# Padding the low part of the attention keys to 128 rows, so that both score passes use one full stationary operand

## The chip, the cores and the metric

The kernel runs on one core of a Trainium2 chip. The metric is device time in microseconds (us) of one execution; the kernel before takes 1814.58 us (median of three runs, 1813.2 to 1815.33). The profiled execution is a separate one; its instructions span 1812.8 us.

## The reference, cut to what matters

A two-layer transformer backbone with 256 context and 256 latent tokens of 1024 features. Each layer is a gated feed-forward step (SwiGLU), a mixer, and a second feed-forward step. The mixer holds four differential-attention heads (each with two queries and two keys of 64 dims), four grouped-query heads (two keys of 64 dims) and a recurrent branch. The part that the change touches is the scores:

```
s1 = einsum('bqhd,bkhd->bhqk', q1, k1) * SCALE      # 64 dims per head
s2 = einsum('bqhd,bkhd->bhqk', q2, k2) * SCALE
p  = softmax(s1) - lam * softmax(s2)                # differential heads
s  = einsum('bqngd,bknd->bngqk', q, k) * SCALE      # grouped-query heads
p  = softmax(s)
```

Latent queries see all 512 keys, context queries the 256 context keys; the second layer has latent queries alone. Everything is float32.

## The kernel before, in words

Activations are kept transposed, features on partitions, tokens along the free axis. Products are made in a reduced-precision matmul type (F32R) from exact splits: a value is a rounded high part plus a low part, and a projection is three matmuls (`mm3`, lines 359 to 362: high by high, low by high, high by low). The stationary operand, which the tensor engine loads by a separate instruction ahead of each matmul, is the first factor.

The mixer (line 502) keeps a pair of 64-dim heads (u = 0 and 1) on the 128 partitions. `stack_q` (L602) makes for each u a 128-row tile that holds the high part of q in the 64 rows of that head and the low part in the other 64. `stack_k` (L611) makes three tiles: for each u the high part of k, written twice (L616 and L617), and one shared tile `k[2]` whose rows 0 to 63 hold the low part for u = 0 and rows 64 to 127 that for u = 1 (L618, on VectorE). `scores` (L665) then adds two matmuls in one PSUM bank: L668 takes all 128 rows and gives (qH + qL) kH; L669 takes the 64 rows of that head alone and gives qH kL:

```
s = acc_bank(1, "s")
own = slice(64 * u, 64 * u + 64)
PE.matmul(s[:, 0:nk], q[u][:, a:a + 128], k[u][:, 0:nk], start=True, stop=False)
PE.matmul(s[:, 0:nk], q[u][own, a:a + 128], k[2][own, 0:nk], start=False, stop=True)
```

One call serves 128 queries of one u against nk = 256 or 512 keys. A differential head makes four calls for each stream of queries (two query tiles by two u), and a grouped-query pass four as well. The first layer has two streams (256 keys for context queries, 512 for latent ones), the second has one, with 512 keys. After a call `softmax` runs a maximum on VectorE (L674), an exponential with its sum on ScalarE (L86, called from L676), and a reciprocal (L677); the differential heads then combine two of these on VectorE (L744 to L746), the grouped-query heads scale (L696). `to_keys` transposes on TensorE (L685) and copies out of PSUM on ScalarE (L686), and the product with the values is L702 or L751.

In each layer the attention falls into three stretches: heads 0 and 1 of the differential attention; the two grouped-query passes; heads 2 and 3. The projections for later heads (tiles `m0vp`, `m0q2p`, `m0k2p`, `m0q3p`, `m0k3p`) and the output projection (`m0oy`) are written so that they fill TensorE's waits. A planner orders each engine's instructions at build time; every engine then runs its list in order. Tiles come from rings set by `TAGS` (L34): six `e` tiles (exponentials), six `Q`, six `K`. Accumulators come from two sets of three PSUM banks; scores use the second.

Of the kernel before, what the change touches and what calls it, by code (L numbers as in the profile page):

```python
# [13 lines left out]
ALU = mybir.AluOpType  # L14
# [18 lines left out]
FSPLIT = (0, 12, 22)  # L33
TAGS = {'e': 6, 'p': 5, 'v': 4, 'Q': 6, 'K': 6, 'o': 8, 'T': 6}  # L34


def shape_constants():
    """Identity, rotary tables on the grid and 0/1 selectors: all from shapes alone."""
    out = np.zeros((128, C_ALL), np.float32)
    out[:, C_IDENT:C_IDENT + 128] = np.eye(128, dtype=np.float32)  # L40
    half = HD // 4
    inv = (np.float32(THETA) ** (-np.arange(half, dtype=np.float32) / np.float32(half))).astype(np.float32)
    t = np.arange(SEQ)
    pos = np.stack([t // GRID_W, t % GRID_W]).astype(np.float32)
    for p in range(128):
        axis, i = (p // 32) % 2, p % 16
        ang = (pos[axis] * inv[i]).astype(np.float32)
        out[p, C_COS:C_COS + SEQ] = np.cos(ang)
        out[p, C_SIN:C_SIN + SEQ] = np.sin(ang) * (-1.0 if p % 32 < 16 else 1.0)
    for h in range(4):  # L50
        out[:, C_LDA + 32 * h + h] = 1.0
    for i in range(3):
        out[:64, C_LGQ + 32 * i + 2 * i] = 1.0
        out[64:, C_LGQ + 32 * i + 2 * i + 1] = 1.0
    return out
# [3 lines left out]
def hybrid_kernel(ctx: ExitStack, tc, x, c, ctx_tok, c_ctx, ada_w, ada_b, norm_g, ffn1_w13, ffn1_w2,  # L59
# [18 lines left out]

    # Functions of one table set stay together: each waits its turn behind the last of the set before it.
    table = {"set": None, "before": None, "last": None}  # L80
# [18 lines left out]
    def acc_bank(which, name):  # L99
        """An accumulator out of one of two sets of banks."""  # L100
        return (psn if which else psm).tile([128, 512], F32, tag="nn" if which else "mm", name=name)
# [8 lines left out]

# [1 line left out]
    cs = cp.tile([128, C_ALL], F32, name="cs")  # L112
# [4 lines left out]

    # small vectors, rows of 128 values turned into columns
    col = {}
# [7 lines left out]
    def columns(pool, base, parts):  # L127
        """Loads rows of 128 and turns them into columns base .. of vT."""
        rows = pool.tile([128, 128], F32, name=f"rows{base}")
# [31 lines left out]

# [1 line left out]
    mods = [cp.tile([128, 72, 2], F32, name=f"mods{l}") for l in range(L)]  # L163
    gs = [cp.tile([128, 3, KD, 2], F32, name=f"gs{l}") for l in range(L)]

    def gain(l, i, k0, k1):
        """(1 + scale) * g of norm i for chunks k0 .. k1-1."""
        n0 = col["ng"] + (3 * l + i) * KD
        V.scalar_tensor_tensor(
            gs[l][:, i, k0:k1], mods[l][:, 8 * (3 * i + 1) + k0:8 * (3 * i + 1) + k1, :], 1.0,  # L170
            vT[:, n0 + k0:n0 + k1].rearrange("p (k o) -> p k o", o=1).to_broadcast([128, k1 - k0, 2]),
            op0=ALU.add, op1=ALU.mult)

    def to_mods(l, acc, m0, mstep, c0, off, what, more=None):
        """Blocks of 512 modulation columns, rows off[block][v] of acc (and those rows + more, a second part of
        the sum), to feature-major with the bias added."""
        nb = len(off)
# [17 lines left out]
    def ada_start(pool, part, acc):  # L195
        """Half of the columns of the first shift and scale, on the tensor engine: the sums."""
        for n in range(4):
# [16 lines left out]
    def ada_mod(pool, l, m):  # L214
        """One modulation vector for both streams: products and sums over row blocks on the vector engine,
        the sum over partitions on the tensor engine."""
        acc = pool.tile([128, 2, 1024], F32, tag="aacc", name=f"aacc{l}_{m}", bufs=1)
# [21 lines left out]

# [1 line left out]
    hT = cp.tile([128, KD, NT], F32, name="hT")  # L241
# [14 lines left out]
    def spread(bc, r, row, n, a, b, r0, r1):  # L256
        """Rows row .. row+n-1 of each token group of r over 128/n partitions each, for tokens a .. b
        (r holds tokens r0 .. r1)."""
        sl = slice(r0 // 4, r1 // 4)
# [8 lines left out]
    class Stat:  # L268
        """Mean square over the features of the residual stream, collected chunk by chunk."""

# [17 lines left out]
        def scales(self, a, b):  # L288
            """1 / rms with tokens on partitions, one column for each 128 of them."""
            nt = (b - a) // 128  # L290
# [23 lines left out]

    # the operand of the products, in two parts whose sum is exact
    xH = xp.tile([128, KD, NT], F32R, name="xH")
    xL = xp.tile([128, KD, NT], F32R, name="xL")

    def modulate(bc, l, i, a, b, k0=0, k1=KD):
        """mod(rmsnorm(h)) of one stream into xH, xL."""  # L320
        v = a // 256
# [7 lines left out]
    class After:  # L329
        """What follows an update of the residual stream: statistics and modulation for the norm  # L330
        nxt = (layer, index)."""

# [9 lines left out]
    def split(src, name, ahead=0):  # L342
        """Exact split of a weight block into its rounded part and the rest."""
        shape = list(src.shape)
# [19 lines left out]
    def load(src, name):  # L364
        """A [128 n, m] block of a weight as [128, n, m]."""
        n, m = src.shape[0] // 128, src.shape[1]
# [9 lines left out]
    def parts_of(c0, cut):  # L376
        """Token ranges for one accumulation: both streams at once or one after the other."""
        if c0 == 0 and cut:
# [3 lines left out]
    def project_back(w, aH, aL, ks, l, gate, c0, nstat, fill, name):  # L382
        """h += gate * (w^T a) for the row blocks ks, and the squares for the next norm."""
        nk = len(ks)
# [32 lines left out]
    def warm(func, src):  # L417
        """Brings a function's table in ahead of its use."""
        d = sml.tile([128, 1], F32, tag="warm", name="warm", bufs=2)
# [63 lines left out]
    def finish_g(accs, gH, gL, f, c0):  # L483
        """silu(a) * b in two parts."""
        (pa, _, _), (pb, _, _) = accs
# [8 lines left out]
    def rope(dst, src):  # L494
        """dst = rotary(src) on [128, SEQ], head dims on partitions."""
        sh = t512("sh")
# [5 lines left out]
    def mixer(l, c0, nstat):  # L502
        W = w_in[l]
        nm = f"m{l}"
        with tc.tile_pool(name=f"mp{l}", bufs=1) as mp, tc.tile_pool(name=f"mt{l}", bufs=1) as mt:
# [18 lines left out]

# [1 line left out]
            bd = mp.tile([128, 2, 2, 2, 128], F32, name="bd")  # L526
# [73 lines left out]

            # Scores in two passes: (qH + qL) kH with both parts of q stacked over the 128 rows, then qH kL.
            def stack_q(t):  # L602
                """qH, qL of rows 0-63 and qL, qH of rows 64-127"""
                q = [m512(f"Q{u}", F32R, "Q") for u in range(2)]
# [6 lines left out]
            def stack_k(t):  # L611
                """kH of rows 0-63, twice, kH of rows 64-127, twice, and kL"""
                k = [m512(f"K{u}", F32R, "K") for u in range(3)]
                for u in range(2):
                    own, other = slice(64 * u, 64 * u + 64), slice(64 - 64 * u, 128 - 64 * u)
                    S.activation(k[u][own], t[own], AF.Copy)  # L616
                    S.activation(k[u][other], t[own], AF.Copy)  # L617
                    V.tensor_tensor(out=k[2][own], in0=t[own], in1=f32(k[u][own]), op=ALU.subtract)  # L618
                return k

            gqa, dq, dk = {}, {}, {}

            # grouped-query heads: tile A holds heads 0 and 2, tile B heads 1 and 3
            def gqa_proj():
# [40 lines left out]
            def scores(q, k, u, a, nk):  # L665
                s = acc_bank(1, "s")
                own = slice(64 * u, 64 * u + 64)
                PE.matmul(s[:, 0:nk], q[u][:, a:a + 128], k[u][:, 0:nk], start=True, stop=False)  # L668
                PE.matmul(s[:, 0:nk], q[u][own, a:a + 128], k[2][own, 0:nk], start=False, stop=True)  # L669
                return s  # L670
# [9 lines left out]
            def to_keys(p, nk):  # L680
                """Probabilities of 128 queries, keys on partitions."""
                tp = ps("tp", "tp")
# [25 lines left out]

            # differential heads
            def qk_load(hp):  # L710
# [60 lines left out]

# [1 line left out]
            raw = load(W[:, 2048:2304], f"{nm}xl")  # L773
# [46 lines left out]

# [1 line left out]
    stat0 = Stat(0, "s0", V)  # L822
# [20 lines left out]
    def small_params():  # L843
        """The vectors that the mixers and the last norm need."""
        base = ng_rows[1]
# [11 lines left out]

        # -lambda of the differential attention, per layer, on all partitions
        lb = t512("lb")
# [14 lines left out]

        # decay constants: -8 softplus(-lambda) and its negative
        lam8 = vT[:, col["lam"]:col["lam"] + 8]
# [32 lines left out]

# [1 line left out]
    outp = ctx.enter_context(tc.tile_pool(name="outp", bufs=1))  # L911
# [50 lines left out]
```

## Time and profile before

| | |
|---|---|
| median of the runs | 1814.58 us |
| span of the profiled execution | 1812.8 us |
| TensorE matmul (PE) busy | 1782.2 us, 98% of the span |
| TensorE weight load (PEld) busy | 1471.9 us, 81% |
| VectorE (DVE) busy | 1131.0 us, 62% |
| ScalarE (ACT) busy | 714.6 us, 39% |
| GpSimd (POOL) busy | 73.7 us, 4% |
| DMA | 249.33 MB, 138 GB/s mean |

The profile gives no time of its own for that execution beside the span, which is 1.8 us shorter than the median of the runs. TensorE overlaps matmuls, so the duration of one matmul is longer than the step from its start to the start of the next; a busy PE says nothing of how dense it works, and the steps between starts are what to read. "Issue" as the cause of an idle gap means that no awaited event explains it.

### The profile page before, as it was taken

The page shows a single profiled execution, that of the slowest core. Times are in us where ns is not written, and L with a number is a line of the kernel's source. Part 1 is how long each engine was busy: PE and PEld are TensorE (multiplying, and loading weights), DVE is VectorE, ACT ScalarE, POOL GpSimd, SP SyncE. Part 2 cuts the span into 40 slices and gives each one's busy share as a digit, 9 for nine tenths or more (in the row PEclk, how much of TensorE's full clock was granted, in tenths as well). Part 3 has the DMA queues.
Part 4 walks back from the last instruction along what each step waited for, and adds up shares of the span by engine and source line. Part 5 has one row for each costly group of instructions (what it writes and reads, how often), then busy time and mean ns, then how long its engine had stood idle before and what let it go on. Part 6 is the DMA issues. An engine that isn't in the chain of part 4 may idle for free.

```text
span 1812.8 us, 23846 instructions
## 1 busy us (share of the span) xinstructions
PE 1782.2 (98%) x9773; PEld 1471.9 (81%) x9773; DVE 1131.0 (62%) x1663; ACT 714.6 (39%) x1131; POOL 73.7 (4%) x67
## 2 busy tenths in 40 slices
PE   6999999999999999999999999999999999999998
PEld 3788888888876788878888898878888877799998
DVE  4767877336757668789566356783333676765554
ACT  3422222325656643222222342222222576754344
POOL 0000000011100010000000100000001010010001
PEclk9999999999999999999999999999999999999999
DMA  9555753232211027557445224552223231135553
GB/s 337 200 177 174 251 202 116 82 105 76 93 43 51 24 85 265 172 175 255 141 150 192 99 94 142 175 171 93 93 82 128 76 107 57 48 121 187 196 163 102
DMA packets 192822, 249.33 MB, mean 138 GB/s; under 512 B 6722, under 2 KB 170952, under 8 KB 192712
## 3 DMA queue, kind: packets, MB, share of 16 engines
q1 hardware_dynamic: 192712, 247.80, 40.3%
q8 instruction: 77, 1.26, 0.3%
q14 instruction: 33, 0.27, 0.0%
HBM read 246.73 MB, written 1.05 MB: 137 GB/s over the span
## 4 chain that ended last, share of the span: by engine, by line
PE 95%; DVE 2%; ACT 1%; issue 1%; DMA 0%; POOL 0%; SPq 0%; ACTq 0%; POOLq 0%; DVEq 0%
PE f_0pa L360 5%; PE f_0pa L361 4%; PE f_0pa L362 4%; PE f_0pb L360 4%; PE f_0pb L361 4%; PE f_0pb L362 4%; PE f_2pa L360 4%; PE f_2pa L361 3%; PE f_2pb L360 3%; PE f_2pa L362 3%; PE f_2pb L361 3%; PE f_2pb L362 3%; PE f_0w0y L360 2%; PE f_0w0y L361 2%; PE f_0w0y L362 2%; PE f_0w1y L360 2%
## 5 line engine op out<-in xcount | busy, mean ns | idle before, releaser
L227 DVE SCALAR_TENSOR_TENSOR aacc<-araw,cpad,aacc 128x1024 f32<-128x1024 f32 x224 | 275.1, 1277 | 2.0 <-DMA araw<-in_ada_w_dram 2.0
L86 ACT ACTIVATE g<-f_0pa 128x512 f32<-128x512 f32 x44 | 26.3, 599 | 154.2 <-PE f_0pa L362 154.2
L488 DVE TENSOR_TENSOR g<-g,f_0pb 128x512 f32<-128x512 f32 x44 | 30.2, 686 | 82.8 <-PE f_0pb L362 72.2
L284 POOL TENSOR_TENSOR sss<-sss,sqs 128x512 f32<-128x512 f32 (+1 forms) x20 | 27.2, 1358 | 1321.1 <-ACT sqs L282 1320.5
L354 DVE TENSOR_TENSOR f_0w_0L<-f_0w,f_0w_0H 128x1024 fp32r<-128x1024 f32 (+1 forms) x32 | 34.7, 1089 | 55.4 <-ACT f_0w_0H L353 55.3
L353 ACT ACTIVATE f_0w_0H<-f_0w 128x1024 fp32r<-128x1024 f32 (+1 forms) x32 | 30.4, 951 | 89.6 <-PE f_0w0y L362 39.8
L86 ACT ACTIVATE g<-f_2pa 128x512 f32<-128x512 f32 (+1 forms) x44 | 21.6, 491 | 108.5 <-PE f_2pa L362 108.4
L354 DVE TENSOR_TENSOR f_2w_0L<-f_2w,f_2w_0H 128x1024 fp32r<-128x1024 f32 (+1 forms) x32 | 34.9, 1090 | 36.0 <-ACT f_2w_0H L353 36.0
L326 ACT ACTIVATE xH<-xn,mods 128x256 fp32r<-128x256 f32 x88 | 39.0, 498 | 43.0 <-DVE xn L325 42.8
L353 ACT ACTIVATE f_2w_0H<-f_2w 128x1024 fp32r<-128x1024 f32 (+1 forms) x32 | 30.4, 951 | 64.2 <-PE f_2w0y L362 30.9
L674 DVE TENSOR_REDUCE sm<-s 128x1 f32<-128x512 f32 (+1 forms) x72 | 42.6, 595 | 17.1 <-PE s L669 16.7
L360 PE MATMUL f_0w0y<-f_0gH,f_0w_0H 128*128 128x512 f32 x128 | 50.6, 397 | 0.0
L361 PE MATMUL f_0w0y<-f_0gH,f_0w_0L 128*128 128x512 f32 x128 | 50.4, 394 | 0.0
L362 PE MATMUL f_0w0y<-f_0gL,f_0w_0H 128*128 128x512 f32 x128 | 50.0, 390 | 0.0
L488 DVE TENSOR_TENSOR g<-g,f_2pb 128x512 f32<-128x512 f32 (+1 forms) x44 | 24.3, 553 | 34.1 <-PE f_2pb L362 29.6
L360 PE MATMUL f_2w0y<-f_2gH,f_2w_0H 128*128 128x512 f32 (+1 forms) x128 | 43.3, 338 | 0.0
L361 PE MATMUL f_2w0y<-f_2gH,f_2w_0L 128*128 128x512 f32 (+1 forms) x128 | 43.1, 336 | 0.0
L362 PE MATMUL f_2w0y<-f_2gL,f_2w_0H 128*128 128x512 f32 (+1 forms) x128 | 42.8, 335 | 0.0
L360 PE MATMUL f_0w1y<-f_0gH,f_0w_0H 128*128 128x512 f32 (+1 forms) x120 | 42.4, 354 | 0.0
L353 ACT ACTIVATE f_0w_4H<-f_0w 128x1024 fp32r<-128x1024 f32 x16 | 17.0, 1060 | 63.7 <-PE f_0w0y L362 26.6
L362 PE MATMUL f_0w1y<-f_0gL,f_0w_0H 128*128 128x512 f32 (+1 forms) x120 | 41.6, 347 | 0.0
L361 PE MATMUL f_0w1y<-f_0gH,f_0w_0L 128*128 128x512 f32 (+1 forms) x120 | 41.6, 347 | 0.0
(1415 smaller groups left out, 5885.5 us busy)
## 6 DMA issues: line engine op xcount, KB each, us to landing
araw<-in_ada_w_dram SPq DMA_DIRECT2D x64, 1024.0 KB
f_0a<-in_ffn_w_dram SPq DMA_DIRECT2D x22, 1024.0 KB
f_0b<-in_ffn_w_dram SPq DMA_DIRECT2D x22, 1024.0 KB
f_2a<-in_ffn_w_dram SPq DMA_DIRECT2D x22, 1024.0 KB
f_2b<-in_ffn_w_dram SPq DMA_DIRECT2D x22, 1024.0 KB
f_0w<-in_ffn_w_dram SPq DMA_DIRECT2D x16, 1024.0 KB
f_2w<-in_ffn_w_dram SPq DMA_DIRECT2D x16, 1024.0 KB
adas<-in_ada_w_dram SPq DMA_DIRECT2D x16, 512.0 KB
```

Of the source, the lines that this page charges most:

```text
L86: i = S.activation(out_, in_, func, **kw)
L227: V.scalar_tensor_tensor(acc[:, v], w[:, i], cpad[:, k, v:v + 1], acc[:, v], op0=ALU.mult, op1=ALU.add)
L284: self.adder.tensor_tensor(out=self.sum[:, a:b], in0=self.sum[:, a:b], in1=sq[:, a:b], op=ALU.add)
L326: S.activation(xH[:, k, a:b], t[:, a:b], AF.Identity, bias=sh)
L353: S.activation(vH, src, AF.Copy)
L354: V.tensor_tensor(out=vL, in0=src, in1=f32(vH), op=ALU.subtract)
L360: PE.matmul(acc, aH, bH, start=first, stop=False)
L361: PE.matmul(acc, aL, bH, start=False, stop=False)
L362: PE.matmul(acc, aH, bL, start=False, stop=last)
L488: V.tensor_tensor(out=t_[:, c0:], in0=t_[:, c0:], in1=pb[:, c0:], op=ALU.mult)
L674: V.reduce_max(st_[:, 0:1], s[:, 0:nk], axis=AX.X, negate=True)
```

## The change

The shared low tile goes. Instead each layer allocates four 128-row tiles `kz` (two sets of two), and GpSimd fills their unused 64 rows with zeros once. `stack_k` takes the sets in turn and writes the low part for u into the 64 rows of that head; the other 64 rows stay zero. The second matmul of `scores` takes the whole 128-row query tile, so the low part of q in the other rows meets zeros, and qH kL is what is added, as before. To make room, the rings of `e` and `Q` go from six to five and that of `K` from six to four (two tiles a call in place of three). The rest of the diff takes comments out.

```diff
-TAGS = {'e': 6, 'p': 5, 'v': 4, 'Q': 6, 'K': 6, 'o': 8, 'T': 6}
+TAGS = {'e': 5, 'p': 5, 'v': 4, 'Q': 5, 'K': 4, 'o': 8, 'T': 6}
...
+            kz = [[mp.tile([128, 512], F32R, name=f"kz{w}{u}") for u in range(2)] for w in range(2)]
+            for w in range(2):
+                for u in range(2):
+                    G.memset(f32(kz[w][u][64 - 64 * u:128 - 64 * u, :]), 0.0)
+            turn = [0]
...
             def stack_k(t):
-                k = [m512(f"K{u}", F32R, "K") for u in range(3)]
+                k = [m512(f"K{u}", F32R, "K") for u in range(2)] + kz[turn[0] % 2]
+                turn[0] += 1
                 for u in range(2):
                     own, other = slice(64 * u, 64 * u + 64), slice(64 - 64 * u, 128 - 64 * u)
                     S.activation(k[u][own], t[own], AF.Copy)
                     S.activation(k[u][other], t[own], AF.Copy)
-                    V.tensor_tensor(out=k[2][own], in0=t[own], in1=f32(k[u][own]), op=ALU.subtract)
+                    V.tensor_tensor(out=k[2 + u][own], in0=t[own], in1=f32(k[u][own]), op=ALU.subtract)
                 return k
...
             def scores(q, k, u, a, nk):
                 s = acc_bank(1, "s")
-                own = slice(64 * u, 64 * u + 64)
                 PE.matmul(s[:, 0:nk], q[u][:, a:a + 128], k[u][:, 0:nk], start=True, stop=False)
-                PE.matmul(s[:, 0:nk], q[u][own, a:a + 128], k[2][own, 0:nk], start=False, stop=True)
+                PE.matmul(s[:, 0:nk], q[u][:, a:a + 128], k[2 + u][:, 0:nk], start=False, stop=True)
                 return s
```

## Rows read from the trace of the kernel before

**Rows 1.** The page: engines' busy time, and the group of score maxima.
```profile
PE 1782.2 (98%) x9773; PEld 1471.9 (81%) x9773; DVE 1131.0 (62%) x1663; ACT 714.6 (39%) x1131; POOL 73.7 (4%) x67
...
L674 DVE TENSOR_REDUCE sm<-s 128x1 f32<-128x512 f32 (+1 forms) x72 | 42.6, 595 | 17.1 <-PE s L669 16.7
```

**Rows 2.** Chain of waits, 500 to 625 us, shares of the stretch by line.
```profile
by line: PE s L669 14.2%; PE s L668 9.6%; PE tp L685 8.1%; PE o L751 7.6%; PE o L702 7.4%; PE m0vp L361 3.9%; PE m0vp L360 3.7%; PE m0vp L362 3.3%; PE m0oy L360 3.0%; PE m0oy L361 2.7%; PE m0oy L362 2.5%; PE m0q3p L361 2.1%; PE m0q3p L362 2
```

**Rows 3.** Timeline, projections of 128 rows (start us, duration us, engine, line, tiles, shape).
```profile
502.88 0.39 PE L361 MATMUL m0gq1p<-xH,m0gq1L 128*128 128x512 f32 x1
502.88 0.19 PEld L362 LDWEIGHTS m0gq1p<-xL,m0gq1H 128*128 128x128 f32 x1
...
503.33 0.39 PE L360 MATMUL m0gq1p<-xH,m0gq1H 128*128 128x512 f32 x1
...
507.25 0.28 PE L362 MATMUL m0vp<-m0v_0L,xH 128*128 128x256 f32 x1
...
507.49 0.28 PE L361 MATMUL m0vp<-m0v_0H,xL 128*128 128x256 f32 x1
```

**Rows 4.** Timeline, one score call of 256 keys and one of 512.
```profile
509.88 0.28 PE L668 MATMUL s<-m0K,m0Q 128*128 128x256 f32 x1
...
510.09 0.38 PE L669 MATMUL s<-m0K,m0Q 64*128 64x256 f32 x1
...
510.62 0.40 PE L668 MATMUL s<-m0K,m0Q 128*128 128x512 f32 x1
...
512.70 0.39 PE L668 MATMUL s<-m0K,m0Q 128*128 128x512 f32 x1
...
513.01 0.18 PEld L669 LDWEIGHTS s<-m0K,m0Q 64*128 64x128 f32 x1 [0.24 <-issue]
513.01 0.50 PE L669 MATMUL s<-m0K,m0Q 64*128 64x512 f32 x1
...
513.44 0.39 PE L361 MATMUL m0vp<-m0v_0H,xL 128*128 128x256 f32 x1
...
513.66 0.28 PE L362 MATMUL m0vp<-m0v_0L,xH 128*128 128x256 f32 x1
```

**Rows 5.** Instructions of L669: durations, and their forms by layer.
```profile
L669 PE MATMUL s<-m0K,m0Q x48: 378/438/502, 505.3 to 619.7; 64*128 64x256 f32 x24, 64*128 64x512 f32 x24
...
L669 PE MATMUL s<-m1K,m1Q x24: 491/498/792, 1494.7 to 1572.8; 64*128 64x512 f32 x24
```

**Rows 6.** Busy time by attention stretch: length, engines in order, clock, DMA.
```profile
505.00:535.00 30.00, 29.90 (x183) 23.17 (x181) 19.54 (x58) 19.05 (x51) 0.00 (x0) 1.00 0.01 2
551.00:585.00 34.00, 33.92 (x183) 21.73 (x184) 25.55 (x65) 23.53 (x58) 1.53 (x2) 1.00 0.09 32
597.00:625.00 28.00, 28.00 (x130) 19.10 (x128) 21.94 (x66) 18.91 (x52) 0.76 (x1) 1.00 0.12 38
1494.00:1518.00 24.00, 24.00 (x138) 18.55 (x140) 13.49 (x31) 14.38 (x32) 0.00 (x0) 0.86 0.12 42
1532.00:1550.00 18.00, 17.66 (x100) 11.18 (x101) 15.50 (x37) 12.88 (x28) 2.19 (x3) 1.00 0.01 1
1562.00:1580.00 18.00, 16.61 (x71) 11.53 (x71) 14.62 (x37) 11.74 (x27) 0.75 (x1) 0.81 0.09 26
```

**Rows 7.** The same view, the two ten-us slices of attention where VectorE is busiest.
```profile
550.00:560.00 10.00, 9.74 (x47) 6.30 (x46) 9.04 (x21) 6.34 (x13) 0.74 (x1) 1.00 0.00 1
1550.00:1560.00 10.00, 10.00 (x72) 7.74 (x70) 9.02 (x19) 8.49 (x21) 0.82 (x1) 1.00 0.31 107
```

**Rows 8.** Timeline of GpSimd at the start of the first mixer.
```profile
421.79 0.95 POOL L527 MEMSET bd<- 128x1024 f32 x1 [15.95 <-PE sts L247]
446.83 1.27 POOL L572 TENSOR_TENSOR m0r<-m0r,m0xc 128x512 f32<-128x512 f32 x1 [24.08 <-ACT m0r L86]
```

**Rows 9.** Timelines: exponentials in the second layer, then query tiles in the first.
```profile
1574.45 0.74 DVE L746 SCALAR_TENSOR_TENSOR m1e<-m1e,sm,m1e 128x512 f32<-128x512 f32 x1
...
1574.57 0.69 ACT L86 ACTIVATE m1e<-s,sm 128x512 f32<-128x512 f32 x1
...
565.71 0.50 PE L669 MATMUL s<-m0K,m0Q 64*128 64x512 f32 x1
...
568.57 1.28 ACT L607 ACTIVATE m0Q<-m0qr 64x512 fp32r<-64x512 f32 x2
```

## The prediction

> **What bounds the kernel now.** I read the page first, then the chain of waits over the attention, then the timeline of TensorE around the two score lines, and last the busy times by stretch. The page says that TensorE has a matmul in flight 98% of the span [rows 1]; no other engine passes 62%. That alone does not show that a shorter matmul shortens the kernel, so the chain is next: between 500 and 625 us it runs through TensorE, and its two largest entries are the score lines, L669 with 14.2% and L668 with 9.6%, together 23.8% of 125 us, 29.8 us [rows 2]. The first layer makes 48 score calls, 24 of 256 keys and 24 of 512; the second makes 24 of 512 [rows 5], 72 in all, which the 72 maxima confirm [rows 1].
>
> How dense could they be? In a run of 128-row matmuls the weight load of the next one starts together with the matmul before it and stands wholly beside it: load at 502.88, matmul at 502.88. From 502.88 to 503.33 there are two steps for 512 columns, 0.225 us each; from 507.25 to 507.49 two for 256 columns, 0.12 us each [rows 3]. At L669 this fails. Its load starts at 513.01, the same moment as its own matmul, after 0.24 us in which the load side sat idle for no awaited event, and the step from L669 to the next matmul is 0.43 us, from 513.01 to 513.44 [rows 4]. The next matmul, again of 128 rows, pays too: 256 columns take 0.22 us (513.44 to 513.66) where 0.12 is normal. The array appears to run empty on the way into the 64-row shape and again on the way out.
>
> **The change part by part: the score passes.** Both passes become 128 rows; the count of matmuls and weight loads and their columns stay. The reader can price one call from start to start:
> - 512 keys: from L668 at 512.70 to the second matmul after the pair at 513.66 is 0.96 us [rows 4]. The same three matmuls at the dense step cost 2 x 0.225 + 0.12 = 0.57 [rows 3]. Saved: 0.39 us.
> - 256 keys: from 509.88 to 510.62 is 0.74 us, against 3 x 0.12 = 0.36. Saved: 0.38 us.
>
> The ceiling is 24 x 0.38 + 48 x 0.39 = 27.8 us, if TensorE alone sets the pace and every pass becomes dense. By layer that is 18.5 and 9.4 us, and by stretch 8 x 0.38 + 8 x 0.39 = 6.2 us in each of the first layer's three and 8 x 0.39 = 3.1 us in each of the second's.
>
> Two statements of the Trainium skill pull apart here. The page "TensorE: Matmul & The Clock Gate", Part 3, section "The mechanism", says that a weight load overlaps matmuls in flight only when the row group differs; by that a full-height load could never hide behind a full-height matmul and the padded pass would gain nothing. The trace of this kernel disagrees, with a 0.19 us load beside a full-height matmul. "TensorEngine Tiling (Array Packing)", section "Key Properties", says that changing the tiling mode drains the engine; by that the drains, 27.8 us at most, are what goes.
>
> **What is late next.** A faster TensorE asks more of VectorE, which carries the maximum, the reciprocal and the combination of every call. Its work in the six attention stretches is unchanged: 19.54 us of 30, 25.55 of 34, 21.94 of 28, then 13.49 of 24, 15.50 of 18 and 14.62 of 18 [rows 6]. The densest slices that the trace shows in attention have VectorE 9.04 and 9.02 us busy in 10 [rows 7], so I let no stretch become shorter than its VectorE work divided by 0.9. That floor leaves room for 30 - 21.7 = 8.3, 34 - 28.4 = 5.6, 28 - 24.4 = 3.6, 24 - 15.0 = 9.0, 18 - 17.2 = 0.8 and 18 - 16.2 = 1.8 us. The gain in a stretch is the smaller of that room and its ceiling: 6.2, 5.6, 3.6, 3.1, 0.8, 1.8. Sum 21.1 us. Where it stops, the late step is a maximum or combination that the transpose behind it waits for. Bounds for the share: at 1.0 the rooms fall short of the ceiling in two stretches alone, 6.1 against 6.2 and 2.5 against 3.1, and the sum is 27.1; at 0.8 the rooms are 5.6, 2.1, 0.6, 7.1, none and none, and the sum is 5.6 + 2.1 + 0.6 + 3.1 = 11.4 us. I take 0.9 because it has been reached in both layers. The matmuls left over in the first layer (projections and output projection) keep TensorE supplied while VectorE catches up, so the floor may be too strict there.
>
> The clock is one term that the sum leaves at zero. The second layer's first and last stretches ran at a mean of 0.86 and 0.81 [rows 6]; with levels of 1.2 and 2.4 GHz that is 24 x 0.14 x 2 = 6.7 us and 18 x 0.19 x 2 = 6.8 us at the lower one, each costing half of that, 3.4 us, if TensorE had work. In the last stretch TensorE also stood idle for 18 - 16.61 = 1.4 us. A denser pass could keep the clock up or, by idling more, lose it once more: bounds -6.8 and +6.8.
>
> **The edits around it.**
> - Zero fills: four per layer on GpSimd. The nearest row is the fill of 128 x 1024 in 0.95 us [rows 8]; a 512-wide tile is half of that at most, 0.48 each, 1.9 us for four. They are queued behind that fill, and the next GpSimd instruction comes after 24.08 us of idleness. Without that cover they would delay L572 by 1.9 us per layer. I take 0, with bounds 0 and 3.8 us in all.
> - `stack_k`: the same two copies and one subtraction per u, in other addresses: 0. A set of `kz` is written again two calls later, just as the ring of six gave three tiles to each of two calls; no new wait.
> - `Q` at five: the third attention projection is stacked at 568.57, after the last scores of the first grouped-query pass, at 565.71 [rows 9]. Until then four of five are in use; the scores just ended give two back, and two are needed: 0. If the order moved it earlier it could wait the 2.9 us between the two rows, while ScalarE goes on with other copies.
> - `e` at five: a sixth exponential is in flight seldom. At 1574.57 one starts while the combination that gives a tile back runs from 1574.45 to 1575.19 [rows 9]; with five tiles it would wait 0.62 us. Behind it on ScalarE stand the copies of transposed tiles, for which the product with the values waits. Value taken: 0, inside the floor above; bounds 0 and 0.62 for each of 24 differential query tiles, 15 us.
>
> **Sum.** The profiled span is 1812.8 us; 1812.8 - 21.1 = 1791.7. The median of the runs is 1.8 us above the span, which I carry over: 1793.5 us.
>
> **The rivals.**
> 1. TensorE stays the only bound in every stretch and the gain is the ceiling: 1814.6 - 27.8 = 1786.8. For it: the chain is TensorE's nearly throughout and filler remains in the first layer. Against: TensorE already idles in the second layer's last stretch.
> 2. The softmax chain takes over earlier, at a VectorE share of 0.8: 1814.6 - 11.4 = 1803.2. For it: the present shares are 0.56 to 0.86, each chain passes between three engines, and the order is fixed at build time. Against: the two slices at 0.9.
> 3. The row count is not what empties the array, for example because the second matmul into the same bank or a load at the same place does. Then nothing moves: 1814.6. Against: the projections also add to one bank, at 0.225 us. By the first skill rule above this would be the outcome.
> 4. Slower, by the ring of five `e` tiles: if exponentials wait for the combination, and the transposed copies queue behind them, each differential query tile (16 in the first layer, 8 in the second) loses a combination and a group of transposes on the path. The combination is 0.74 us; with an exponential of 0.69 us repeated behind it, 1.43 us [rows 9]. All 24 would cost 34 us and give 1814.6 - 27.8 + 34 = 1821. It beats the forecast gain from 15 tiles on (21.1 / 1.43). Against: few exponentials need the sixth tile today.
>
> **How the numbers follow.** Chances: forecast 0.58, its own range 1788 to 1799; rival 1 0.15; rival 2 0.18; rival 3 0.04; rival 4 0.05. Of the ceiling and a clock that stays up I take in half the clock's bound: 1786.8 less 3 is 1784. On the other side the range reaches past rival 2 to 1806, a further 2.8 us for one more clock fall. A measurement of this kernel can tell about 0.2%, 3.6 us, from no change. Faster: 0.58 + 0.15 + 0.18 = 0.91; the same 0.04; slower 0.05.
>
> **What would show it.** In the profile after, L669 should read 128 x 256 and 128 x 512 with its load ahead of its matmul and steps of 0.12 and 0.225 us; the idle "issue" before L669 should go. The chain's share of the two score lines should fall from 29.8 us towards 48 calls x 2 dense passes, 24 x 0.24 + 24 x 0.45 = 16.6 us. VectorE's share in the third and the last two stretches should rise to 0.9 and waits of TensorE for VectorE or ScalarE appear there. If the steps stay at 0.43 the mechanism is wrong; if they fall and the stretches do not shorten, the floor is; if waits for an `e` tile lead ScalarE's list, rival 4 is what happened.

## The result and the profile after

The changed kernel takes 1787.75 us (median of four runs, 1787.57 to 1788.57), the kernel before 1814.86 beside it: ratio 0.9852, 95% interval 0.9838 to 0.9866, so 27 us less. Forecast were 1793.5 us, a range of 1784 to 1806, and 1788 to 1799 for the forecast's own case. A later comparison of the same pair gave 1788.64 against 1815.1, ratio 0.9855 (0.984 to 0.987). The profiled execution spans 1786.0 us against 1812.8, 26.8 us less.

The page after, which answers to [rows 1]: TensorE lost 29 us of busy time, VectorE next to nothing (1.6 us), and the number of matmuls is the same.

```profile
PE 1753.0 (98%) x9773; PEld 1465.0 (82%) x9773; DVE 1129.4 (63%) x1663; ACT 714.0 (40%) x1131; POOL 77.7 (4%) x75
```

The timeline of the two score lines after (L668 is now L675, L669 now L676), for [rows 4]. L675 and L676 at 509.64 and 509.86 are a call of 256 keys, those at 511.49 and 511.72 a call of 512.

```profile
509.64 0.39 PE L675 MATMUL s<-m0K,m0Q 128*128 128x256 f32 x1
...
509.86 0.28 PE L676 MATMUL s<-kz,m0Q 128*128 128x256 f32 x1
509.86 0.19 PEld L360 LDWEIGHTS m0vp<-m0v_0H,xH 128*128 128x128 f32 x1
509.98 0.28 PE L360 MATMUL m0vp<-m0v_0H,xH 128*128 128x256 f32 x1
...
511.49 0.39 PE L675 MATMUL s<-m0K,m0Q 128*128 128x512 f32 x1
511.50 0.19 PEld L676 LDWEIGHTS s<-kz,m0Q 128*128 128x128 f32 x1
511.72 0.39 PE L676 MATMUL s<-kz,m0Q 128*128 128x512 f32 x1
511.73 0.19 PEld L361 LDWEIGHTS m0vp<-m0v_0H,xL 128*128 128x128 f32 x1
511.95 0.28 PE L361 MATMUL m0vp<-m0v_0H,xL 128*128 128x256 f32 x1
...
512.07 0.28 PE L362 MATMUL m0vp<-m0v_0L,xH 128*128 128x256 f32 x1
```

The reader is to see the load of L676 at 511.50, beside the matmul that starts at 511.49 and not behind it, and the steps: 0.23 and 0.23 us for the pair, 0.12 for the next matmul. From 511.49 to 512.07 it is 0.58 us where [rows 4] had 0.96, so 0.38 less. (The call of 256 keys shown begins after 0.19 us of waiting for ScalarE, and its first step is 0.22; over the first layer's 24 such calls the median steps are 0.12 and 0.12.) The chain of waits over the attention, for [rows 2], now from 500 to 610 us: the score lines fell from 29.8 us to (8.1% + 6.8%) of 110 us, 16.4 us.

```profile
by line: PE tp L692 9.5%; PE o L758 9.2%; PE s L675 8.1%; PE o L709 8.1%; PE s L676 6.8%; PE m0vp L360 3.6%; PE m0vp L362 3.5%; PE m0vp L361 3.5%; PE m0k3p L361 2.2%; PE m0oy L362 1.9%; PE m0gbc L265 1.9%; PE m0q3p L362 1.9%; PE m0q3p L360 
```

The six stretches after, cut to whole microseconds at about the places of [rows 6], with nearly the same number of VectorE's instructions in each (start and end; length; PE, PEld, DVE, ACT and POOL busy; TensorE's clock, as the mean granted share of 2.4 GHz; DMA):

```profile
505.00:530.00 25.00, 24.96 (x186) 22.80 (x184) 19.12 (x58) 18.49 (x51) 0.00 (x0) 1.00 0.04 13
544.00:574.00 30.00, 29.52 (x197) 21.34 (x195) 25.97 (x68) 24.52 (x59) 2.21 (x3) 1.00 0.11 36
586.00:609.00 23.00, 22.34 (x130) 18.06 (x129) 21.54 (x66) 18.73 (x50) 0.75 (x1) 1.00 0.14 46
1477.00:1497.00 20.00, 18.65 (x144) 17.06 (x145) 14.00 (x32) 14.99 (x33) 0.00 (x0) 1.00 0.17 53
1511.00:1527.00 16.00, 15.75 (x108) 11.76 (x109) 15.29 (x37) 12.75 (x27) 1.84 (x3) 1.00 0.01 2
1538.00:1555.00 17.00, 14.37 (x95) 11.53 (x91) 14.58 (x37) 13.63 (x30) 0.75 (x1) 1.00 0.10 30
```

They are 131 us where they were 152, so 21 us less: 5, 4, 5, 4, 2 and 1. The cuts matter here: from the first score to the last product with the values the last stretch takes 21.9 us before (1562.3 to 1584.2) and 18.1 after (1538.7 to 1556.8), 3.8 us less and not 1. VectorE's share rose to 0.94 in the third and 0.96 in the fifth, and TensorE has more idle time than before, 2.6 us of it in the last where [rows 6] had 1.4, behind ScalarE's exponentials and copies. Two things beside the lengths differ: the clock column reads 1.00 in all six where it had read 0.86 and 0.81, and 26.8 - 21 = 5.8 us went outside the stretches.

By layer, from the first projection of one mixer to that of the next: the first mixer starts 0.7 us later than before (417.8 and 418.5), the second 15.8 us earlier (1418.5 and 1402.7), as the rows of those tiles show, before and after in turn (count, duration in ns as least, median and most, first and last start, shape):

```profile
L360 PE MATMUL m0xlp<-xH,m0xl0H x16: 278/283/387, 417.8 to 433.8; 128*128 128x256 f32 x16
L360 PE MATMUL m1xlp<-xH,m1xl0H x16: 278/283/388, 1418.5 to 1434.5; 128*128 128x256 f32 x16
```
```profile
L360 PE MATMUL m0xlp<-xH,m0xl0H x16: 278/283/387, 418.5 to 434.5; 128*128 128x256 f32 x16
L360 PE MATMUL m1xlp<-xH,m1xl0H x16: 278/283/387, 1402.7 to 1418.7; 128*128 128x256 f32 x16
```

So the first layer gave 16.5 us (forecast 15.4, ceiling 18.5) and everything from the second mixer on 26.8 - 15.8 = 11.0 us (forecast 5.7, ceiling 9.4). More than the ceiling of the steps can't all come from the steps. The excess lies inside the second mixer: from its first projection to the last matmul of its output projection (`m1oy`, rows before and after) it takes 186.8 us before (1418.5 to 1605.3) and 175.4 after (1402.7 to 1578.0, from unrounded times), 11.4 us less.

```profile
L362 PE MATMUL m1oy<-xL,m1o_4H x32: 277/283/362, 1581.3 to 1605.3; 128*128 128x256 f32 x32
```
```profile
L362 PE MATMUL m1oy<-xL,m1o_4H x32: 278/283/388, 1554.0 to 1578.0; 128*128 128x256 f32 x32
```

### The profile page after: what moved, and what is told of

It reads as the page before. It is cut to its first block, busy times and chain, and to the rows that moved or that the text cites. A ratio compares the mean times of both kernels' runs of the same rounds, so it can differ in the third digit from the quotient of the medians.

```text
span 1786.0 us, 23865 instructions
## 1 busy us (share of the span) xinstructions
PE 1753.0 (98%) x9773; PEld 1465.0 (82%) x9773; DVE 1129.4 (63%) x1663; ACT 714.0 (40%) x1131; POOL 77.7 (4%) x75
## 4 chain that ended last, share of the span: by engine, by line
PE 94%; DVE 2%; ACT 2%; issue 1%; DMA 0%; POOL 0%; SPq 0%; ACTq 0%; POOLq 0%; DVEq 0%
PE f_0pa L360 5%; PE f_0pa L361 5%; PE f_0pb L360 5%; PE f_0pa L362 5%; PE f_0pb L361 4%; PE f_0pb L362 4%; PE f_2pa L360 4%; PE f_2pb L360 3%; PE f_2pa L361 3%; PE f_2pa L362 3%; PE f_2pb L361 3%; PE f_2pb L362 3%; PE f_0w0y L360 3%; PE f_0w0y L362 2%; PE f_0w0y L361 2%; PE f_0w1y L360 2%
```

## The experiments

**The second pass over 64 rows again, all else as changed.**

```diff
-PE.matmul(s[:, 0:nk], q[u][:, a:a + 128], k[2 + u][:, 0:nk], start=False, stop=True)
+PE.matmul(s[:, 0:nk], q[u][own, a:a + 128], k[2 + u][own, 0:nk], start=False, stop=True)
```

> The changed kernel with the second score pass taken over the 64 rows of its head again; the padded tiles, the zero fills and the shorter rings stay. Theory (the price is the change between the 64-row and the 128-row shape): the steps of the second pass go back from 0.12 and 0.225 us to 0.31 and 0.43 us, and the time to 1814.6, within 3 us of the kernel before. Rival (the gain came from the rings, the placement of the tiles or another order of the work): the time stays within 3 us of 1787.75.

Measured: 1813.01 us against 1816.01, ratio 0.9984 (0.9974 to 0.9993). The steps are back:

```profile
513.45 0.39 PE L675 MATMUL s<-m0K,m0Q 128*128 128x512 f32 x1
513.77 0.50 PE L677 MATMUL s<-kz,m0Q 64*128 64x512 f32 x1
514.20 0.39 PE L361 MATMUL m0vp<-m0v_0H,xL 128*128 128x256 f32 x1
514.42 0.28 PE L362 MATMUL m0vp<-m0v_0L,xH 128*128 128x256 f32 x1
```

With everything else of the change in place, nearly the whole gain is gone. A small remainder, 0.16%, 2.9 us, stays.

**The shape alone, in the kernel before.**

```diff
-PE.matmul(s[:, 0:nk], q[u][own, a:a + 128], k[2][own, 0:nk], start=False, stop=True)
+PE.matmul(s[:, 0:nk], q[u][:, a:a + 128], k[2][:, 0:nk], start=False, stop=True)
```

> The kernel before with the shape of the second pass alone changed: it takes the whole query tile against the whole shared low tile, so the low part of the other head's keys adds a wrong term to the scores. Rings, tiles, zero fills and copies are those of the kernel before. Theory (the shape is the whole cause; shorter rings, zero fills and moved tiles cost nothing): the time of the changed kernel, 1788.6 within 1.5 us. Rivals: shorter rings cost something now that TensorE is faster, then 1784 to 1787; or part of the gain came from the new tiles (two low tiles in place of a shared one), then above 1791.

Measured: 1791.3 us against 1815.62, ratio 0.9867 (0.9852 to 0.9882), 24 us less. The steps are those of the changed kernel:

```profile
511.24 0.39 PE L668 MATMUL s<-m0K,m0Q 128*128 128x512 f32 x1
511.47 0.39 PE L669 MATMUL s<-m0K,m0Q 128*128 128x512 f32 x1
511.70 0.28 PE L361 MATMUL m0vp<-m0v_0H,xL 128*128 128x256 f32 x1
511.82 0.28 PE L362 MATMUL m0vp<-m0v_0L,xH 128*128 128x256 f32 x1
```

The time is above the 1.5 us allowed for "the whole cause", on the side of the last rival. The four corners fit together: 0.9984 x 0.9867 = 0.9851, and the whole change measured 0.9852 and 0.9855. So the shape gives some 24 us and the tiles, rings and fills with the order that the planner makes of them some 2 to 3. Which of them gives these was not separated. The traces say where they arise: with the fills, tiles and rings the first mixer, cut as the second was above, is 1.3 us shorter in the pair with 64 rows (249.7 and 248.4) and 1.5 in the pair with 128 (234.6 and 233.1), at a granted clock of 1.00 in all four, so that part isn't the clock. The second mixer is 1.1 us shorter (186.8 and 185.7) and 2.1 (177.4 and 175.4); there the clock differs as well, since this run has short falls in the second layer's attention (0.87 from 1480 to 1490 us and again from 1540 to 1550) where the first profile of the changed kernel reads 1.00.

**Two calls issued together, 64-row passes.**

```diff
+                ss = [acc_bank(1, "s") for _ in qu]
+                for s, (q, u) in zip(ss, qu):
+                    PE.matmul(s[:, 0:nk], q[u][:, a:a + 128], k[u][:, 0:nk], start=True, stop=False)
+                for s, (q, u) in zip(ss, qu):
+                    own = slice(64 * u, 64 * u + 64)
+                    PE.matmul(s[:, 0:nk], q[u][own, a:a + 128], k[2 + u][own, 0:nk], start=False, stop=True)
```

> The 64-row second pass again, but two score calls are issued together: two 128-row passes, then two 64-row passes, each pair into two banks. 72 calls become 36 pairs. Theory (the price is paid once per change of shape): half of it goes, some 14 us, so about 1801 us, and the step between two adjacent 64-row passes is near 0.225 us for 512 keys. Rival (each 64-row pass costs 0.2 us in itself, whatever stands beside it): as with single calls, 1811 to 1815 us, and the step between adjacent 64-row passes is 0.43 us.

Measured: 1806.83 us, ratio 0.9953 (0.9938 to 0.9968); between both expectations. In the trace the planner had taken nearly all pairs apart: 5 of 36 have their 64-row passes side by side. Those five start 3 to 4 ns apart, against an expected 0.225 us. As a test of the price it was inconclusive, and why it is 6 us faster than single calls with so few pairs stays open (its trace also lacks the later of the two clock falls met below, with 1.00 from 1500 to 1600 us); it was repeated with the order held.

**The same with the order held.** A dependency without a wait makes both 64-row passes follow the second 128-row pass, and a higher priority keeps them together; the trace has all 36 pairs side by side.

> As in the pairs before, the 64-row second pass with two calls issued together, but the order is now held: two 128-row passes come before two 64-row passes with nothing between these. For a differential pair the two 64-row passes take different halves of the rows, for a grouped-query pair the same half. In the earlier run the few such passes that stood side by side in different halves started 3 to 4 ns apart. Theory (the price is paid per change of shape, and passes in different row halves run side by side): a differential pair costs 0.18 us beyond dense streaming in place of 0.78, a grouped-query pair 0.39 in place of 0.78; 24 x 0.60 + 12 x 0.39 = 19 us less than the unpaired 64-row passes (1813 us), so 1794, between 1791 and 1799. Rival (each 64-row pass costs 0.39 us wherever it stands): 1811 to 1815.

Measured: 1798.44 us, ratio 0.9907 (0.9891 to 0.9924). Within the theory's bounds and 12.6 us or more from the rival. Timeline of TensorE, a pair of each length; "x2" stands for two matmuls:

```profile
511.65 0.50 PE L684 MATMUL s<-kz,m0Q 64*128 64x512 f32 x2
512.09 0.50 PE L680 MATMUL s<-m0K,m0Q 128*128 128x512 f32 x1
...
518.70 0.38 PE L684 MATMUL s<-kz,m0Q 64*128 64x256 f32 x2
```

Two 512-column passes on different row halves together take from 511.65 to 512.09, 0.44 us, where one alone took 0.43 in [rows 4]. All 24 differential pairs start 3 ns apart (median); the 12 grouped-query pairs, on the same rows, step by 0.22 us (256 keys) and 0.34 (512). The number of 64-row passes is that of the kernel before, and more than half of their price is gone (1798.4 us, with 1813.0 for single calls and 1787.8 for padding). So most of the price belongs to the change of shape and the stretch in which half the rows stand empty. Not all of it: on the same rows the second 64-row pass, with no change of shape before it, still steps by 0.22 and 0.34 us where 128 rows step by 0.12 and 0.225. Padding is still 10 us better than pairs.

**Padding once more, in columns.** The grouped-query values get zero columns, so that the product has a 128-column stationary operand. A second fill on GpSimd clears the tile, and the ring of `T` goes from six to five for room.

```diff
-PE.matmul(o[64 * u:64 * u + 64, 128 * qt:128 * qt + 128], gvs[0][:, ... 64 columns ...],
+PE.matmul(o[:, 128 * qt:128 * qt + 128], gz[:, b0:b0 + 128],   # [values | 0] or [0 | values]
```

> The changed kernel, and the same padding once more at the product of the grouped-query probabilities with their values: its 64-column stationary operand is widened by 64 zero columns to 128, both heads adding into one 128-row result. In the profile of the changed kernel the steps into and out of that shape cost 1.78 + 1.98 us in the first layer and 1.01 + 1.13 us in the second beyond streaming. Theory (a change of shape costs in columns as in rows, and TensorE still sets the pace): 3 to 6 us less than 1787.75, so 1782 to 1785. Rival (the softmax chain on VectorE and ScalarE now sets these stretches): 1787 to 1789, with more idle time of TensorE behind ScalarE.

Measured: 1790.14 us, ratio 0.9856 (0.9841 to 0.9871): no gain over 0.9852. The steps at the edges became shorter, as expected (behind a transpose 0.20 us before, 0.11 now), but the theory had missed what stood inside. Here are the first layer's groups of this product, of the changed kernel and then of this one:

```profile
563.13 1.09 PE L709 MATMUL o<-m0pT,m0gv 128*64 128x128 f32 x14
```
```profile
565.23 1.83 PE L712 MATMUL o<-m0pT,gz 128*128 128x128 f32 x14 [0.24 <-ACT m0pT L695]
```

Fourteen matmuls take 1.09 us narrow and 1.83 us wide. The narrow ones of the two heads write different column halves and start in pairs, 6 to 7 ns apart with 0.10 to 0.16 us to the next pair; the wide ones step by 0.11 us each. Padding lost the company that these matmuls had: over the 138 steps from one to the next the mean went from 0.071 to 0.120 us, 6.8 us in all, more than the 5.9 us that the edges had cost. The rival's reason, a softmax chain that takes over, isn't needed for the missing gain, but it is not out: this product waited 4.1 us for transposed probabilities where it had waited 0.7.

**VectorE: six low-part subtractions moved to GpSimd.**

```diff
-V.tensor_tensor(out=xL[:, m, c0:], ...)
+(V if m in (2, 3) else G).tensor_tensor(out=xL[:, m, c0:], ...)
```

> The changed kernel with six of the eight low-part subtractions of the output projection's input per layer moved from VectorE to GpSimd, which takes about 4 us in the first layer and 2.5 us in the second off VectorE, most of it in the attention's last stretches. Theory (VectorE limits these stretches): 1 to 3 us less than 1787.75. Rival (TensorE alone sets the pace, or ScalarE does): within 1 us of it.

Measured: 1791.06 us, ratio 0.9862 (0.9846 to 0.9879): no gain, if anything a loss. It is inconclusive on VectorE, because the subtraction of 128 x 512 takes 1.30 to 1.50 us there against 0.69 and its results come later. In its trace the first mixer is 3.8 us longer than in the changed kernel (236.9 and 233.1) and the second 1.2 shorter (174.2 and 175.4).

**VectorE: the scaling of probabilities left out.**

```diff
-V.tensor_scalar(e[:, 0:nk], e[:, 0:nk], st_[:, 2:3], None, op0=ALU.mult)      # grouped-query
-V.tensor_scalar(e2[:, 0:nk], e2[:, 0:nk], s2[:, 3:4], None, op0=ALU.mult)     # differential
```

> The changed kernel without the scaling of the probabilities by VectorE: the multiplication by the reciprocal is left out for the grouped-query heads, and that of the second softmax for the differential heads, 48 of some 0.35 to 0.49 us, 21 us of VectorE work in the six stretches, which also shortens each softmax chain by one step. Theory (VectorE and its chain hold the time above TensorE's own pace): 3 to 6 us less than the changed kernel. Rival (TensorE alone sets it): within 1 us.

Measured: 1786.87 us, ratio 0.9843 (0.9829 to 0.9856), beside the changed kernel's 1788.64 and 0.9855. That is 1.8 us, between both expectations. VectorE is busy 18 us less (1111.9 and 1129.7 us, in the profiles of this run and of the changed kernel beside it; 21 were expected), and the whole bought some 2. The sum hides two parts: the second mixer is 3.1 us shorter (172.5 and 175.6), so there VectorE and its chain do hold the time; the first is 1.3 longer (234.5 and 233.2), and why isn't shown.

The yardstick for this run and two others:

> The changed kernel itself, beside the three below on one chip, so that they have a yardstick there: 1786 to 1790 us, and a mean granted clock of 0.993 to 0.995 as in its four runs, against 0.990 to 0.992 in the kernel before.

It gave the 1788.64 us above and a mean granted clock of 0.994 in its profile.

**Seven exponential tiles in place of five.** The rings of `v` and `T` give up one tile each for them.

```diff
-TAGS = {'e': 5, 'p': 5, 'v': 4, 'Q': 5, 'K': 4, 'o': 8, 'T': 6}
+TAGS = {'e': 7, 'p': 5, 'v': 3, 'Q': 5, 'K': 4, 'o': 8, 'T': 5}
```

> The changed kernel with seven exponential tiles in place of five; the room comes from the recurrent branch's weight tile, which is free by then and takes the grouped-query values and one tile of the differential values (rings of v at three and of T at five). In the trace of the changed kernel ScalarE waits 1.3 us and 2.4 us in the two layers for a combination to give an exponential tile back. Theory (the short ring holds TensorE up): 1 to 3 us less than the changed kernel, and those waits gone. Rival (they are hidden): within 1 us.

Measured: 1789.3 us, ratio 0.9857 (0.9843 to 0.987): the same as 0.9855. ScalarE's waits of the changed kernel for a combination (L753) to give a tile back,

```profile
ACT m0e L86 <- DVE m0e L753: 1.3, 3, 0.5
```

do not occur in its trace any more, and the time does not move. They are hidden; the fourth rival of the prediction is out.

**The clock, in the kernel before.**

```diff
+if l == 1:
+    dm = ps(f"dm{i}")
+    for n in range(16 if i else 8):
+        PE.matmul(dm[:, 0:256], xH[:, n % 8, 0:128], xH[:, n % 8, 256:512], ...)
```

> The kernel before with 8 and 16 extra matmuls of 256 columns (0.12 us each, results unused) in the second layer behind the two grouped-query query projections, where TensorE idles 1.36 and 1.99 us ahead of the first attention stretch and its clock falls to a mean of 0.76 over the next 10 us. Theory (the clock's fall is on the path and the change removed it): the clock of the slices from 1490 to 1510 us stays at 1.00 and the time falls by 1.5 to 3.5 us. Rival (the softmax chain sets the pace there, so the clock costs nothing): within 1 us of the kernel before, or up to 1 us slower by extra matmuls that miss the gaps.

Measured: 1813.42 us against 1815.1, ratio 0.9989 (0.998 to 0.9998), 1.7 us less by the medians. These are the slices of the kernel before in which the clock fell during the second layer's attention:

```profile
1490.00:1500.00 10.00, 8.01 (x35) 5.58 (x35) 7.48 (x10) 9.79 (x18) 0.00 (x0) 0.76 0.30 105
1500.00:1510.00 10.00, 10.00 (x51) 7.33 (x50) 6.07 (x18) 4.35 (x11) 0.00 (x0) 0.89 0.01 2
1570.00:1580.00 10.00, 10.00 (x48) 8.08 (x48) 8.03 (x22) 4.21 (x11) 0.00 (x0) 0.66 0.15 45
```

In this run the first two read 1.00 (the later fall stays, here seen over 40 us):

```profile
1490.00:1500.00 10.00, 9.84 (x63) 7.71 (x61) 7.51 (x10) 9.26 (x18) 0.00 (x0) 1.00 0.32 107
1500.00:1510.00 10.00, 10.00 (x60) 7.49 (x60) 8.26 (x24) 6.02 (x16) 0.00 (x0) 1.00 0.00 0
1560.00:1600.00 40.00, 38.61 (x253) 32.11 (x253) 27.49 (x54) 23.84 (x47) 7.29 (x6) 0.91 0.25 80
```

Twenty-four matmuls of useless work made the kernel faster, if only just clear of noise, so the fall was on the path. The median hides two groups. Of the eleven executions of this one program the five with a mean clock of 0.994 over the whole execution, the profiled one among them, took 1811.0 to 1812.0 us, and the four at 0.992 took 1814.2 to 1814.9; the two at 0.993 lie between, at about 1813.4. Between the two groups lie 2.8 us, with no difference in the program; only one of the eleven has a profile, so that it is this fall which sets them apart is inferred. In the profiled execution of the changed kernel the same stretch keeps its clock without such help:

```profile
1480.00:1520.00 40.00, 38.53 (x282) 32.48 (x281) 30.78 (x70) 27.97 (x58) 3.21 (x4) 1.00 0.19 64
```

Not in every execution: the profile of its repeat, the yardstick above, has part of the first fall, though its second mixer is hardly longer for it (175.6 us and 175.4); the later fall is absent there too (1.00 from 1520 to 1560 us).

```profile
1470.00:1480.00 10.00, 7.35 (x46) 6.57 (x46) 7.91 (x13) 9.25 (x17) 0.00 (x0) 0.89 0.30 99
1480.00:1490.00 10.00, 10.00 (x71) 9.33 (x70) 9.40 (x25) 7.88 (x20) 0.00 (x0) 0.93 0.03 9
```

## Why the prediction was right, and where it was not

The direction, the mechanism and the price of a call were right. The load now stands beside the matmul before it, the steps are 0.12 and 0.23 us, a call of 512 keys with the matmul behind it costs 0.38 us less (0.39 said), and the score lines' share of the chain is 16.4 us (16.6 said). Undone, the gain goes; done alone, it comes to 24 us. Rival 3, that the row count is not what empties the array, is out. The trace thereby also decides between the two statements of the Trainium skill that the prediction weighed. It agrees with the Trainium skill's "TensorEngine Tiling (Array Packing)", section "Key Properties", in which a change of the tiling mode drains the engine: the change cost 0.38 us a call. It disagrees with the sentence of the Trainium skill's "TensorE: Matmul & The Clock Gate", Part 3, "The mechanism", that asks for another row group: a full-height load does hide behind a full-height matmul (511.50 beside 511.49). The prediction read that section more strictly than it stands, since its opening also allows the background weight buffer beside another row group.

What was off is size: 21.1 us said, 27 measured, just below the 1788 to 1799 us of the forecast's own case. Two terms that the sum left at zero account for it as far as the runs show.

- The clock, taken at 0 between bounds of -6.8 and +6.8. It went toward the lower bound: of the two falls of the second layer's attention both are gone in one profile of the changed kernel, and the later one and part of the first in the other. Kept up by other means in the kernel before, the first alone is worth 1.7 us by the medians and 2.8 between executions of one program with and without the higher clock. If the later fall cost as much, as an estimate, the 11.4 us of the second mixer less twice 2.8 leave 5.8, about the 5.7 forecast for its steps. That the clock is where the excess over the ceiling comes from is therefore likely, but not shown: the later fall was not tried, and the repeat with part of the first fall was no slower.
- The tiles and rings, each taken at 0 or as a possible loss. Together with the new order they gave 2 to 3 us, in both pairs of kernels that differ in them alone, 1.3 and 1.5 of them in the first mixer, where the clock doesn't fall. The cause of that part stays open; the rest, in the second layer, can't be told from the clock.

The floor of VectorE's work over 0.9 held worse than its sum. The stretches shortened by 21 us as said, but 5 + 4 + 5 + 4 + 2 + 1 are not 6.2, 5.6, 3.6, 3.1, 0.8 and 1.8: the third and fifth passed the floor (0.94 and 0.96), the fourth passed even its ceiling, with a clock that rose from 0.86 to 1.00, and the first two came short of what they were given. Taking 18 us of VectorE's work away gave 1.8 us, while the floor took 27.8 - 21.1 = 6.7 us off the ceiling. So the agreement of the sums is in part luck: the floor was too strict in some stretches and the clock uncounted, the first two fell short by 2.8 us, and the whole-microsecond cuts decide how much the last one gave. Rival 1 (1786.8) came closest to the measured time, with the right sum for a partly wrong reason: TensorE did not stay the only bound, it idles 2.6 us in the last stretch, and the order, and likely the clock, made up for it.

The shorter ring of exponentials costs nothing, as said, and with all fills and rings in place the 64-row kernel was not slower. A fill takes 0.52 us where the prediction allowed 0.48 at most; it falls into idle time of GpSimd, as said.

## What to carry to other kernels

Look at where weight loads start: one that started together with its own matmul, after idle time with no awaited event, between loads that start one matmul early, marked a change of the array's shape in this kernel, and the step to the next start priced it. Padding to the full shape paid where narrow matmuls stood alone between full ones; where narrow ones of different halves already stood side by side, padding took their company away and gave the gain back. When a denser TensorE is forecast, count the stretches at the lower clock as part of what can be won.

## What the runs showed of the hardware that was not expected

- Two 64-row matmuls on different row halves started 3 ns apart and together took 0.44 us for 512 columns, where one alone took 0.43; on the same half they stepped by 0.34 us, and 128-row ones by 0.225.
- Two 64-column matmuls on different column halves started 6 to 7 ns apart; widened to 128 columns they stepped by 0.11 us.
- Eight and sixteen unused matmuls in idle gaps of 1.36 and 1.99 us kept the granted clock at 1.00 over the next 20 us of the profiled execution, where it had been 0.76 and 0.89, and made the kernel 1.7 us faster by the medians.
